# A three-mixer decoder trunk: the attention's mask moved from TensorE to VectorE, the opening's norm in other tiles, HGRN2's tail in a pool at the other end of SBUF

## The chip, the core and the metric

The kernel runs on one core of a Trainium2 chip. The core has five engines, each with its own instruction queue worked in order: TensorE (PE: matrix products, with the weight loads shown apart as PEld), VectorE (DVE), ScalarE (ACT), GpSimd (POOL) and SyncE (SP), whose queue mostly issues DMA transfers. Data lie in SBUF, 128 partitions wide; matrix products land in PSUM, which has eight banks of 128 x 512 float32 here. The metric is the device time in microseconds of one execution; a version's time is the median of several runs.

## The reference

Two layers, each: half a SwiGLU feed-forward step, a mixing step with three parallel mixers, half a second SwiGLU step. Model width 1024, sequence 512, hidden width 2816, all float32.

```python
def rms_norm(x, gain):
    inv = lax.rsqrt(jnp.mean(xf * xf, axis=-1, keepdims=True) + EPS)
    return (xf * inv) * gain

def swiglu(h, w_in, w_out):
    gate, up = jnp.split(h @ w_in, 2, axis=-1)
    return (jax.nn.silu(gate) * up) @ w_out

def fox_mixer(q, k, v, f_logit, f_bias, q_gain, k_gain):    # 8 heads of 64
    qh = rms_norm(heads(q), q_gain) * (HEAD_DIM ** -0.5)
    kh = rms_norm(heads(k), k_gain)
    cum = jnp.cumsum(jax.nn.log_sigmoid(f_logit + f_bias), axis=1)
    # block i of 128 queries:
    s = qh_i @ kh.T + (cum_i[:, None] - cum[None, :])
    s = jnp.where(qpos >= kpos, s, -1e30)
    o_i = softmax(s) @ vh

for l in range(DEPTH):
    x = x + 0.5 * swiglu(rms_norm(x, ffn1_norm[l]), ffn1_w_in[l], ffn1_w_out[l])
    h = rms_norm(x, mix_norm[l]) @ w_mix_in[l]              # 3336 columns, split over the mixers
    y = concat[short_conv(...), hgrn2(...), fox_mixer(...)] # widths 256, 256, 512
    x = x + y @ w_mix_out[l]
    x = x + 0.5 * swiglu(rms_norm(x, ffn2_norm[l]), ffn2_w_in[l], ffn2_w_out[l])
```

The short convolution is causal with three taps and two gates. HGRN2 is a gated linear recurrence with four heads, worked in chunks of 64 steps, whose output is normed per head (a mean of squares), scaled by a gain and gated by a SiLU.

## The kernel before, in words

Activations lie transposed in SBUF: features on partitions, the 512 tokens along the free dimension. A float32 product is made of three products of parts in a TensorE format: a value is split into a high part (a cast on ScalarE) and a low part (a subtraction on VectorE), and high x high, high x low and low x high are added in one PSUM bank (`mm3`, lines 318, 324, 325). Weights of the dense products come by SP into a staging tile `st` (two buffers), are split into a tile `hl` (three buffers; lines 307 and 308), and TensorE works through a stream of such pieces.

*Opening.* The first feed-forward step reads x as it arrives. `open_stream` (lines 1710 and around) turns x and works the first product while x and its weights land; the sum of squares `sqa` runs along on VectorE. Behind it the norm is made in `end_norm`: the sum is split in two tiles `sh` (`parted_norm`, line 421), summed over partitions by a product with a matrix of ones (line 430) into a bank, and ScalarE and VectorE make the reciprocal root from it (tiles `nr` and `nt`, then `inv`). Dense products use x without the norm and are multiplied by `inv` when their bank is cleared, so the second product needs no `inv`. Behind the norm `lower_bounds` loads the logits of HGRN2's lower bound by SP (line 956) into a tile `lb`. The tiles `sh` and `lb` share the tag `g1`, with two buffers. SP's loads around here stand in a written-out order, the logits' load in front of the second product's weights.

*Mixing step.* Its projections come first; those of HGRN2 lie in a pool `hg` with its working tiles, and HGRN2 runs as a generator beside the projections of the attention (`fox_qkv`): after each part of HGRN2, some pieces of dense work are recorded. Its end is the mean of squares of its output (line 1402, banks `pt`), two multiplications per half (line 1409), then five operations of VectorE over 1024 columns (lines 1412 to 1421). `fox_decay` makes the cumulated log gates with eight products (line 1440) into a `pt` bank. Then the pool closes and a pool `at` for the attention opens in its place.

The attention (`fox_attend`) runs twice, over four heads each, beside dense work: the convolution's projections and gates with the first four heads, six eighths of the output product with the last four. A head is prepared by `fox_prep` (line 1495 transposes, 1498 to 1506 splits, plus three small DMA transfers on SP and a POOL memset at 1492), then has four items, one per block of 128 queries, with 128 to 512 keys each. An item is: two products of scores into an `sc` bank (lines 1521, 1522), one that adds the mask (line 1523: an identity times a 128 x 128 matrix with -1e30 above the diagonal), the negated row maximum by VectorE (1526), Exp by ScalarE with that maximum as bias and the row sum beside it, reciprocal and scaling, transposes of the weights into a `pt` bank (1584), a split of them (1586, 1587) and products with V (1543). Scores are recorded three items ahead (`LOOK`); the tile `P`, which holds an item's Exp, has three buffers.

What sets the order: program text is recorded, and a scheduler orders each engine's instructions by the order of recording, the dependencies and its own estimates, except where the code fixes a chain with `follow`. Pools hand their space to the next pool when they close.

Of the kernel before, what the change touches and what calls it, by code (L numbers as in the profile page):

```python
# [8 lines left out]
F32 = mybir.dt.float32  # L9
# [14 lines left out]
P = 128  # L24
# [132 lines left out]
class Trunk:  # L157
# [32 lines left out]
    def build_consts(self, scratch):  # L190
# [19 lines left out]
        self.identb = c.tile([P, P], BF16, tag="identb", name="identb")  # L210
        nc.vector.tensor_copy(self.identb, self.ident)
# [206 lines left out]
    def parted_norm(self, pool, tag, bufs, keep=False):  # L418
        nc = self.nc
        hi, lo = (pool.tile([P, T], F32R, tag=tag, name=self.n("sh"), bufs=bufs) for _ in range(2))  # L420
        a, b = nc.scalar.copy(hi, self.sqacc), nc.vector.tensor_sub(lo, self.sqacc, hi)
        if keep:
            self.follow("a", a)
            self.follow("v", b)
        return hi, lo
# [133 lines left out]
    def enter(self, fp, w_in, then):  # L559
# [18 lines left out]
        parts = self.parted_norm(fp, "g1", 2, True)  # L578
# [420 lines left out]
    def mix(self, l, w, w_out, conv_w, out_gain, q_gain, k_gain, f_bias, next_gain):  # L999
# [3 lines left out]
        with tc.tile_pool(name=self.n("mix"), bufs=1) as mp:  # L1003
# [6 lines left out]
            self.mp = mp  # L1010
            og, qkg, fb, cw = col("og", 1), col("qkg", 1), col("fb", NH), col("cw", 6)
# [39 lines left out]
            with tc.tile_pool(name=self.n("hg"), bufs=1) as hp:  # L1051
                self.tt, self.tb = "t", 3
                norm = lambda: self.end_norm(
                    self.bank("pt"), hp, self.parted_norm(hp, self.tt, self.tb)
                )
                bz = features([(H_F, 256)], ("mm", "mm"), norm)
                bg = features([(H_G, 256)], ("mm", "po"))
                inv = self.inv
                z, q, sg = (
                    hp.tile([P, 2, T], F32, tag=t, name=self.n(t)) for t in ("z", "q", "sg")  # L1060
                )
                for i in range(2):
                    nc.vector.tensor_mul(z[:, i, :], bz[i], inv)
                for i in range(2):
                    nc.vector.tensor_mul(sg[:, i, :], bg[i], inv)
                self.table(SILU)
                self.act(sg, sg, AF.Silu)
                self.table(LNEXP)

                ib = hp.tile([P, 4, P], F32, tag="t", name=self.n("ib"), bufs=self.tb)  # L1070
                self.invc, self.inv2 = col("invc", 4), col("inv2", 4)
                nc.vector.tensor_mul(
                    ib, inv.rearrange("p (i t) -> p i t", i=4),
# [712 lines left out]
```

## Time and profile before

| | us |
|---|---|
| median of 3 runs | 1832.18 |
| lowest, highest | 1830.63, 1835.08 |
| the profiled execution | 1827.76 |
| its span (first to last instruction) | 1826.0 |
| TensorE busy | 1809.0 (99%) |
| VectorE busy | 1466.3 (80%) |
| ScalarE busy | 989.9 (54%) |
| mean granted TensorE clock | 0.998 |

The profile is of one execution. A line such as "L1526 DVE TENSOR_REDUCE nm<-sc" names the source line, the engine, the operation, the tile written and the tile read. The idle time behind a bar or in brackets is that of the engine just before the instruction, with what ended it. Records of matmuls overlap: one of 512 columns is shown 0.39 us long, and the next can start 0.23 us after it. The opening lies at 0 to 38 us, the mixing steps at about 390 to 600 us and 1290 to 1500 us.

### The profile page before, as it was taken

How to read it: one execution, taken by the hardware profiler on the slowest of the kernel's cores; microseconds unless marked ns; L12 is line 12 of the kernel's file. 1: busy time of each engine (PE TensorE's matmuls, PEld its weight loads, DVE VectorE, ACT ScalarE, POOL GpSimd, SP SyncE). 2: the span in 40 equal slices, each digit the busy share in tenths (PEclk: the TensorE clock that was granted, in tenths of full speed). 3: DMA queues.
4: the chain of work that ended last, by engine and by line, in shares of the span. 5: the costliest groups of instructions: out<-in, count | busy, mean ns of one | idle time of the engine just before them, and what ended most of it. 6: DMA issues, size and time to landing. Idle time of an engine off the chain costs nothing.

```text
span 1826.0 us, 34831 instructions
## 1 busy us (share of the span) xinstructions
PE 1809.0 (99%) x14345; PEld 1684.3 (92%) x14345; DVE 1466.3 (80%) x2017; ACT 989.9 (54%) x1402; POOL 169.5 (9%) x168
## 2 busy tenths in 40 slices
PE   8999999999999999999999999999999999999999
PEld 6899999899878899999889999998997788999997
DVE  8788888676797988879678887866858878888883
ACT  5455555454675565555445555555547665555551
POOL 0011020100000001112001111201000000020210
PEclk9999999999999999999999999999999999999999
DMA  5849684233322767868265787813333228677762
GB/s 147 233 109 199 171 174 113 70 88 83 87 71 92 216 141 163 191 168 174 81 193 137 162 191 194 165 64 82 83 82 82 76 93 231 162 152 195 153 137 92
DMA packets 243935, 250.94 MB, mean 137 GB/s; under 512 B 18457, under 2 KB 229153, under 8 KB 243777
## 3 DMA queue, kind: packets, MB, share of 16 engines
q1 hardware_dynamic: 189872, 182.38, 32.8%
q0 software_dynamic: 53600, 66.09, 22.7%
q8 instruction: 112, 1.84, 0.4%
q14 instruction: 47, 0.38, 0.1%
q10 hardware_dynamic: 304, 0.27, 0.0%
HBM read 223.98 MB, written 2.10 MB: 124 GB/s over the span
## 4 chain that ended last, share of the span: by engine, by line
PE 92%; DVE 3%; ACT 3%; DMA 1%; issue 1%; SPq 0%; ACTq 0%; DVEq 0%
PE mm L318 13%; PE mm L325 13%; PE mm L324 13%; PE sc L325 6%; PE sc L324 6%; PE sc L318 6%; PE pt L318 6%; PE pt L324 6%; PE pt L325 6%; PE po L318 3%; PE po L324 3%; PE po L325 3%; PE po L1543 1%; PE sc L1710 1%; PE pt L1710 1%
## 5 line engine op out<-in xcount | busy, mean ns | idle before, releaser
L786 ACT CAST hl<-w 128x1024 fp32r<-128x1024 f32 x322 | 337.5, 1051 | 317.9 <-PE mm L325 76.8
L788 DVE TENSOR_TENSOR hl<-w,hl 128x1024 fp32r<-128x1024 f32 x322 | 392.7, 1222 | 85.8 <-ACT hl L786 85.6
L307 ACT CAST hl<-st 128x512 fp32r<-128x512 f32 (+2 forms) x188 | 142.2, 756 | 190.3 <-PE po L325 67.8
L308 DVE TENSOR_TENSOR hl<-st,hl 128x512 fp32r<-128x512 f32 (+2 forms) x188 | 161.6, 860 | 100.3 <-ACT hl L307 98.6
L318 PE MATMUL mm<-xc,hl 128*128 128x256 f32 (+1 forms) x732 | 201.7, 276 | 0.5 <-ACT g L897 0.5
L325 PE MATMUL mm<-xc,hl 128*128 128x256 f32 x728 | 201.6, 277 | 0.0
L324 PE MATMUL mm<-xc,hl 128*128 128x256 f32 x728 | 201.5, 277 | 0.0
L325 PE MATMUL sc<-xc,hl 128*128 128x256 f32 x528 | 146.0, 277 | 0.0
L318 PE MATMUL sc<-xc,hl 128*128 128x256 f32 (+1 forms) x530 | 146.0, 276 | 0.0
L324 PE MATMUL sc<-xc,hl 128*128 128x256 f32 x528 | 145.9, 276 | 0.0
L318 PEld LDWEIGHTS mm<-xc,hl 128*128 128x128 f32 x732 | 137.3, 188 | 0.8 <-ACT g L897 0.7
L324 PEld LDWEIGHTS mm<-xc,hl 128*128 128x128 f32 x728 | 137.0, 188 | 0.0
L325 PEld LDWEIGHTS mm<-xc,hl 128*128 128x128 f32 x728 | 136.7, 188 | 0.1
L318 PE MATMUL pt<-xc,hl 128*128 128x256 f32 (+1 forms) x484 | 132.9, 276 | 0.0
L324 PE MATMUL pt<-xc,hl 128*128 128x256 f32 x480 | 132.7, 277 | 0.0
L325 PE MATMUL pt<-xc,hl 128*128 128x256 f32 x480 | 132.5, 276 | 0.0
L318 PE MATMUL mm<-x,hl 128*128 128x512 f32 x272 | 108.5, 399 | 6.0 <-ACT hl L307 5.6
L324 PE MATMUL mm<-x,hl 128*128 128x512 f32 x272 | 107.5, 395 | 0.0
L325 PE MATMUL mm<-x,hl 128*128 128x512 f32 x272 | 107.1, 394 | 0.0
L318 PEld LDWEIGHTS sc<-xc,hl 128*128 128x128 f32 x530 | 99.5, 188 | 0.2
L325 PEld LDWEIGHTS sc<-xc,hl 128*128 128x128 f32 x528 | 99.1, 188 | 0.1
L324 PEld LDWEIGHTS sc<-xc,hl 128*128 128x128 f32 x528 | 99.1, 188 | 0.0
(510 smaller groups left out, 5618.2 us busy)
## 6 DMA issues: line engine op xcount, KB each, us to landing
w<-in_ffn_w_in_dram SPq DMA_DIRECT2D x140, 512.0 KB, 5.2
w<-in_ffn_w_out_dram SPq DMA_DIRECT2D x64, 512.0 KB, 4.5
w<-in_ffn_w_out_dram POOLq DMA_DIRECT2D x56, 512.0 KB, 8.6
st<-in_w_mix_in_dram SPq DMA_DIRECT2D x88, 256.0 KB, 2.7
st<-in_ffn_w_in_dram SPq DMA_DIRECT2D x70, 256.0 KB, 3.3
w<-in_ffn_w_in_dram POOLq DMA_DIRECT2D x35, 512.0 KB, 8.5
w<-S POOLq DMA_DIRECT2D x35, 512.0 KB, 4.8
st<-in_ffn_w_out_dram SPq DMA_DIRECT2D x24, 512.0 KB, 4.6
```

Of the source, the lines that this page charges most:

```text
L307: a = nc.scalar.copy(hi, src[:, c : c + w])
L308: b = nc.vector.tensor_sub(lo, src[:, c : c + w], hi)
L318: i = nc.tensor.matmul(acc[:, c], ah, bh[:, c], start=first and c.start == 0, stop=False, skip_group_check=True,)
L324: nc.tensor.matmul(acc, ah, bl, start=False, stop=False, skip_group_check=True)
L325: i = nc.tensor.matmul(acc, al, bh, start=False, stop=last, skip_group_check=True)
L786: A(nc.scalar.copy(hi, src))
L788: return lambda: V(nc.vector.tensor_sub(lo, src, hi))
L1543: nc.tensor.matmul(self.ob[:, t0 + u * P : t0 + 2 * P], V[:, j, h % 4].rearrange("p a d -> p (a d)"), part[:, j, u:, :].rearrange("p i t - ...
L1710: E(nc.tensor.matmul(acc, wh[j][l][:, cols], (self.xh, self.xl)[r][k + j], start=k + j == 0 and which == 0, stop=k + j == KD - 1 and which ...
```

## The change

Four things change.

1. The opening's norm takes its two tiles `sh` from the tags `r0` and `r1` (one buffer each) and no longer from `g1`; `lb` stays in `g1`.
2. The mask's product and its identity go. A tile `zmask`, zeros and then the mask's 128 columns, is made once per layer by POOL, and VectorE's `tensor_tensor_reduce` adds the end of it to the scores, writes the negated sum into `P` and keeps the running minimum, which is the negated maximum. ScalarE's Exp reads `P` with scale -1 and no longer the bank. The operation is built as two instructions, the second of which writes the minimum.
3. HGRN2's last tiles (its four temporaries `T` and the gate `sg`) lie in a pool `hb` at SBUF's other end, its mean uses `sc` banks, and it stops once more, right after the two multiplications of line 1409. There the pool `hg` closes and the attention's pool opens in its place; its tiles wait for the tiles that they overlap and not for a whole pool. HGRN2's five last operations are recorded when the attention's fourth item is reached, and the tiles of the attention's results come in a pool `fy` in `hb`'s place after that.
4. `fox_decay` is recorded at HGRN2's first stop, and the first two heads are prepared before the last projections.

```diff
-    def parted_norm(self, pool, tag, bufs, keep=False):
+    def parted_norm(self, pool, tags, bufs, keep=False):
...
-        hi, lo = (pool.tile([P, T], F32R, tag=tag, name=self.n("sh"), bufs=bufs) for _ in range(2))
+        hi, lo = (pool.tile([P, T], F32R, tag=tag, name=self.n("sh"), bufs=bufs) for tag in tags)
...
-                    self.parted_norm(fp, "g1", 2),
+                    self.parted_norm(fp, ("r0", "r1"), 1),
...
+            self.zmask = mp.tile([P, T], BF16, tag="zm", name=self.n("zm"))
+            nc.gpsimd.memset(self.zmask[:, : T - P], 0.0)
+            nc.gpsimd.tensor_copy(self.zmask[:, T - P :], self.maskb)
...
+            left, right = ExitStack(), ExitStack()
+            hp = left.enter_context(tc.tile_pool(name=self.n("hg"), bufs=1))
+            hb = right.enter_context(tc.tile_pool(name=self.n("hb"), bufs=1, side="right"))
...
+            hgrn = self.hgrn(l, hp, hb, z, q, v, sg, og)
+            for part, n in enumerate(hgrn):
+                if n is None:
+                    break
+                if part == 0:
+                    self.fox_decay(mp, zf)
+                for _ in range(n):
+                    next(dense, None)
+            left.close()
+            ap1 = left.enter_context(
+                tc.tile_pool(name=self.n("at"), bufs=1, reuse_waits="tile")
+            )
+            for tag in ("PH", "PL"):
+                ap1.tile([P, 4, 2, P], F32R, tag=tag, name=self.n(tag), bufs=2)
+            ops = {h: self.fox_prep(ap1, h, half[0][0], qkg) for h in range(2)}
+            for _ in dense:
+                pass
...
+            def finish():
+                nonlocal ap2
+                for _ in hgrn:
+                    pass
+                right.close()
+                ap2 = right.enter_context(
+                    tc.tile_pool(name=self.n("fy"), bufs=1, side="right", reuse_waits="tile")
+                )
...
+            def beside(attend, dense, then=()):
+                for n, _ in enumerate(attend):
+                    if n == 3 and then:
+                        then()
+                    if n >= 2:
                         next(dense, None)
                 for _ in dense:
                     pass
...
+            beside(self.fox_attend(ap1, 0, half[0], qkg, ops), conv(), finish)
+            beside(self.fox_attend(ap1, 1, half[1], qkg, {}), most())
...
-        tmp = lambda: hp.tile([P, W], F32, tag="T", name=self.n("T"), bufs=4)
+        tmp = lambda: hb.tile([P, W], F32, tag="T", name=self.n("T"), bufs=4)
...
-        mb = [self.bank("pt") for _ in range(2)]
+        mb = [self.bank("sc") for _ in range(2)]
...
+        yield None
         nc.vector.tensor_scalar(t, t, scalar1=-0.5, scalar2=1.5, op0=ALU.mult, op1=ALU.add)
...
-            nc.tensor.matmul(sb[:, :n], QB[:, c], KB[:, :n], start=False, stop=False)
-            nc.tensor.matmul(sb[:, c], self.identb, self.maskb, start=False, stop=True)
+            nc.tensor.matmul(sb[:, :n], QB[:, c], KB[:, :n], start=False, stop=True)
...
-            nc.vector.tensor_reduce(nm, sb[:, :n], axis=AX.X, op=ALU.max, negate=True)
             pb = tl("P", 3)
-            self.act(pb[:, :n], sb[:, :n], AF.Exp, bias=nm, accum_out=rs)
+            nc.vector.tensor_tensor_reduce(
+                pb[:, :n], sb[:, :n], self.zmask[:, T - n :], -1.0, 3e38, ALU.add, ALU.min, nm
+            )
+            self.act(pb[:, :n], pb[:, :n], AF.Exp, bias=nm, scale=-1.0, accum_out=rs)
```

How this moves instructions is seen on three engines' queues. SP at the end of the opening, with the semaphores that each row waits for (a name such as DVE_49 is the counter of that engine, DMAHW a transfer's): before, the logits' load (`lb`), then the second product's weights (`st_504`):

```order
L1657 DMA st_296<-in_ffn_w_in_dram 128x2x256 [waits DMAHW3_49]
L956 DMA lb_457<-in_hgrn_lb_logits_dram 128x4x1 [waits DMAHW4_49,DVE_49,PE_49]
L290 DMA st_504<-in_ffn_w_in_dram 128x2x256 [waits DMAHW7_49,DMAHW6_49,DMAHW5_49]
L290 DMA st_504<-in_ffn_w_in_dram 128x2x256
L290 DMA st_534<-in_ffn_w_in_dram 128x2x256 [waits DMAHW3_49,DMAHW2_49]
```

After the change, at the same place of SP's queue:

```order
L1687 DMA st_296<-in_ffn_w_in_dram 128x2x256 [waits DMAHW3_49]
L954 DMA lb_455<-in_hgrn_lb_logits_dram 128x4x1 [waits DMAHW4_49]
L288 DMA st_502<-in_ffn_w_in_dram 128x2x256 [waits DMAHW6_49,DMAHW7_49,DMAHW5_49,DVE_49]
L288 DMA st_502<-in_ffn_w_in_dram 128x2x256
L288 DMA st_532<-in_ffn_w_in_dram 128x2x256 [waits DMAHW6_49,DMAHW5_49,DVE_49]
```

The logits' load waits for no engine any more; the weights behind it wait for VectorE's last reading of their buffer.

TensorE there: before, the opening's last products (`pt_83`), the norm's two (`po_410`), then the second product (`mm_500`):

```order
L1710 MATMUL pt_83<-x_47_300,hl_299 128x512 x3
L1710 MATMUL pt_83<-x_48_305,hl_299 128x512 x3
L430 MATMUL po_410<-sh_411,ones_mean 128x512
L430 MATMUL po_410<-sh_412,ones_mean 128x512
L318 MATMUL mm_500<-x_18_120,hl_507 128x512
```

After, from the opening's last four blocks on:

```order
L1740 MATMUL sc_80<-x_48_305,hl_299 128x512
L316 MATMUL mm_498<-x_18_120,hl_505 128x512
L322 MATMUL mm_498<-x_18_120,hl_505 128x512
L323 MATMUL mm_498<-x_18_120,hl_505 128x512
L316 MATMUL mm_499<-x_18_120,hl_505 128x512
...
L1740 MATMUL pt_83<-x_47_300,hl_299 128x512 x3
L1740 MATMUL pt_83<-x_48_305,hl_299 128x512 x3
L428 MATMUL po_408<-sh_409,ones_mean 128x512
L316 MATMUL mm_500<-x_18_120,hl_505 128x512
L428 MATMUL po_408<-sh_410,ones_mean 128x512
```

Products of the second step stand among those of the opening, and one between the norm's two.

VectorE at the attention's first items, before (`nm` the maximum, `PL` a low part, `hl` a weight's):

```order
L1529 RECIPROCAL rs_5468<-rs_5468 128x1
L1587 TENSOR_TENSOR PL_5503<-pt_5504,PH_5502 128x128
L1533 TENSOR_SCALAR P_5470<-P_5470,rs_5468 128x384
L1529 RECIPROCAL rs_5496<-rs_5496 128x1
L1526 TENSOR_REDUCE nm_5512<-sc_5508 128x1
L1587 TENSOR_TENSOR PL_5503<-pt_5519,PH_5502 128x2x128
```

After, at the same items:

```order
L1617 TENSOR_TENSOR PL_5488<-pt_5489,PH_5487 128x128
L1554 ISA P_5498,nm_5496<-sc_5493,zm_3718 128x128
L1554 ISA nm_5496 128x1
L1617 TENSOR_TENSOR PL_5488<-pt_5503,PH_5487 128x2x128
L1558 RECIPROCAL rs_5481<-rs_5481 128x1
L1441 TENSOR_TENSOR T_5240<-T_5240,T_5241 128x1024
L306 TENSOR_TENSOR hl_5757<-st_5754,hl_5757 128x512
```

The maximum has become two instructions, and HGRN2's last operations (`T`, line 1441 of the changed file) stand between the items.

TensorE at the decay, before: after the last projection's piece (`po_5242`) and the first of the convolution (`mm_5525`) come the eight products into `pt_5388`, then the first head's transposes:

```order
L325 MATMUL po_5242<-hl_5351,x_404_3711 128x256
L325 MATMUL mm_5525<-x_379_3569,hl_5529 128x512
L1440 MATMUL pt_5388<-utri,flh_5384 8x512
L1440 MATMUL pt_5388<-utri,fll_5385 8x512
...
L1440 MATMUL pt_5388<-utri,fll_5385 8x128
```

After, they stand some 900 rows earlier, in front of HGRN2's first transposes (`pt_4201`), among the attention's first projection (`mm_4167`):

```order
L322 MATMUL mm_4167<-hl_4170,x_381_3573 128x256
L1468 MATMUL pt_4153<-utri,flh_4149 8x512
L1468 MATMUL pt_4153<-utri,fll_4150 8x512
...
L1468 MATMUL pt_4153<-utri,fll_4150 8x128
L323 MATMUL mm_4167<-hl_4170,x_381_3573 128x256
L1280 MATMUL pt_4201<-ident,T_4197 128x128 x4
```

The two heads' transposes now follow HGRN2's mean directly.

More of the change, by code (lines that the diff above doesn't have):

```diff
@@ new lines, in mix @@
+            inv = self.inv
+            z, q = (hp.tile([P, 2, T], F32, tag=t, name=self.n(t)) for t in ("z", "q"))
+            sg = hb.tile([P, 2, T], F32, tag="sg", name=self.n("sg"))
+            for i in range(2):
+                nc.vector.tensor_mul(z[:, i, :], bz[i], inv)
+            for i in range(2):
+                nc.vector.tensor_mul(sg[:, i, :], bg[i], inv)
+            self.table(SILU)
+            self.act(sg, sg, AF.Silu)
+            self.table(LNEXP)
+            ib = hp.tile([P, 4, P], F32, tag="t", name=self.n("ib"), bufs=self.tb)
@@ new lines, in mix, with projections @@
+            half = [{}, {}]
+            def projections():
+                for hf in range(2):
+                    yield from self.fox_qkv(mp, hf, tokens, half)
+            dense = projections()
+            hgrn = self.hgrn(l, hp, hb, z, q, v, sg, og)
[6 more added lines that the diff above has]
+                    next(dense, None)
```

195 lines of the change are left out of this document (84 added, 111 removed).

## The prediction

> **What bounds the kernel now.** I read the profile's page first, then what TensorE waited for, then a table by stage, then the timeline at the places the change touches.
>
> ```profile
> span 1826.0 us, 34831 instructions
> ...
> PE 1809.0 (99%) x14345; PEld 1684.3 (92%) x14345; DVE 1466.3 (80%) x2017; ACT 989.9 (54%) x1402; POOL 169.5 (9%) x168
> ...
> PE 92%; DVE 3%; ACT 3%; DMA 1%; issue 1%; SPq 0%; ACTq 0%; DVEq 0%
> ...
> PE mm L318 <- ACT hl L307: 5.6, 1, 5.6
> PE pt L1440 <- DVE T L1409: 1.6, 2, 0.8
> PE mm L318 <- ACT cy L1181: 0.5, 2, 0.2
> ```
>
> TensorE carries the time: busy 99%, 92% of the chain that ended last. A change can win in two ways only, by fewer matmuls or by waits of TensorE. The largest wait is one of 5.6 us, in front of a dense product. The table by stage (PE, PEld, DVE, ACT and POOL busy, then the granted clock, DMA share and GB/s) shows where it lies, and how full VectorE is around the attention of layer 0 (layer 1 reads alike):
>
> ```profile
> 33.00:38.00 5.00, 0.00 (x0) 0.00 (x0) 3.21 (x10) 2.56 (x5) 0.00 (x0) 0.65 0.74 209
> 38.00:42.00 4.00, 3.92 (x10) 2.97 (x11) 3.82 (x6) 2.21 (x4) 0.00 (x0) 0.58 0.39 115
> 42.00:61.00 19.00, 19.00 (x85) 15.73 (x84) 17.16 (x33) 7.17 (x7) 1.44 (x1) 1.00 0.94 254
> ...
> 460.00:487.00 27.00, 26.22 (x167) 22.61 (x166) 19.48 (x33) 16.98 (x28) 0.99 (x2) 1.00 0.31 77
> 487.00:547.00 60.00, 58.77 (x340) 45.73 (x339) 55.94 (x131) 44.89 (x108) 3.24 (x6) 1.00 0.30 79
> 547.00:590.00 43.00, 42.57 (x227) 34.22 (x226) 30.40 (x62) 23.26 (x49) 0.00 (x0) 1.00 0.32 101
> ```
>
> From 33 to 38 us TensorE does nothing, and until 42 its clock is 0.58. In the attention's first 60 us VectorE is busy 93% and TensorE idles 1.23 us; ahead of it VectorE has 7.52 us free, behind it 12.6.
>
> **The opening.** The engines' timeline, SP's queue first:
>
> ```profile
> 14.96 0.88 SPq L1657 DMA_DIRECT2D st<-in_ffn_w_in_dram  x2
> 32.30 0.37 SPq L956 DMA_DIRECT2D lb<-in_hgrn_lb_logits_dram  x1
> 32.78 9.16 SPq L290 DMA_DIRECT2D st<-in_ffn_w_in_dram  x8
> ...
> SPq L956 <- DVE sh L421: 15.7, 1, 15.7
> ...
> DMA to landing us min/median/max: 2.9/3.4/7.6
> ...
> 19.99 0.67 DVE L1667 TENSOR_TENSOR hl<-st,hl 128x512 fp32r<-128x512 f32 x1
> 26.68 0.68 DVE L1667 TENSOR_TENSOR hl<-st,hl 128x512 fp32r<-128x512 f32 x1
> 30.87 0.69 DVE L421 TENSOR_TENSOR sh<-sqa,sh 128x512 fp32r<-128x512 f32 x1 [0.32 <-ACT sh L421]
> 34.64 0.69 DVE L414 SCALAR_TENSOR_TENSOR nt<-po,nt 128x512 f32<-128x512 f32 x1 [3.08 <-ACT nt L270]
> 36.98 1.05 ACT L307 CAST hl<-st 128x1024 fp32r<-128x1024 f32 x1 [2.38 <-DMA st<-in_ffn_w_in_dram]
> 38.06 1.23 DVE L308 TENSOR_TENSOR hl<-st,hl 128x1024 fp32r<-128x1024 f32 x1 [0.21 <-ACT hl L307]
> ...
> 31.87 0.63 PE L430 MATMUL po<-sh,ones_mean 128*128 128x512 f32 x2
> 38.08 0.80 PE L318 MATMUL mm<-x,hl 128*128 128x512 f32 x1 [5.58 <-ACT hl L307]
> 38.68 0.63 PE L324 MATMUL mm<-x,hl 128*128 128x512 f32 x1
> 39.10 0.63 PE L318 MATMUL mm<-x,hl 128*128 128x512 f32 x1
> 41.54 0.40 PE L325 MATMUL mm<-x,hl 128*128 128x512 f32 x1
> 41.77 0.40 PE L318 MATMUL po<-x,hl 128*128 128x512 f32 x1
> ...
> 84.57 1.23 DVE L788 TENSOR_TENSOR hl<-S,hl 128x1024 fp32r<-128x1024 f32 x1 [4.21 <-ACT hl L786]
> ```
>
> SP's queue stands from 15.9 to 32.3 on the logits' load, whose tile has the norm's buffer (tag g1), and the next weights stand behind it. They land at about 36, and TensorE idles 5.58 us. Then the clock is low: eight matmuls start from 38.08 to 41.54, in 3.46 us, where steps of 0.23 (41.54 to 41.77) would take 1.84. That is 1.6 us more, 7.2 together.
>
> With the norm in r0 and r1 the logits wait for no norm. The weights' buffer is free at 20.66 (19.99 + 0.67); 3.4 later they have landed, at 24.1, and cast (1.05) and low part (1.23) are done by about 27, while TensorE is at the opening's product until 31.87. So the whole 5.58 goes, and seven matmuls of the second product even stand ahead of the norm's second. What is late next is the norm. On VectorE its low part now stands behind that of the following weights, whose buffer comes free with the opening's last low part (27.36, and 1.23 later for the one put in front: 28.6). They land at 32.0, are cast at 33.0, lowered at 34.3, and the norm's low part ends near 35.0. TensorE arrives at 31.87 plus seven steps, 33.5. So 1.5 us of waiting come back; the rows show a low clock behind 5.58 us of idling alone, so I count it as gone. Opening: 7.2 - 1.5 = 5.7 us less. Ends: 7.2 where nothing waits; 3 where the reciprocal norm, some 3.5 us later than now, holds the banks of the third product too. I take 5.7, since VectorE's own idle of 3.08 and 4.21 us in these rows lets it come that much earlier.
>
> [...]
>
> **The mask.** 64 matmuls go, and the maximum becomes an addition with a running minimum, with a second instruction that reads it out.
>
> ```profile
> 489.06 0.23 PE L1523 MATMUL sc<-maskb,identb 128*128 128x128 bf16 x1
> 489.10 0.36 PE L1521 MATMUL sc<-KA,QA 128*128 128x256 f32 x1
> 490.62 0.23 PE L1523 MATMUL sc<-maskb,identb 128*128 128x128 bf16 x1
> 490.78 0.30 PE L1584 MATMUL pt<-ident,P 128*128 128x128 f32 x1
> 474.53 0.66 PE L1495 MATMUL pt<-ident,qk 128*128 128x128 f32 x4
> ...
> L1526 DVE TENSOR_REDUCE nm<-sc 128x1 f32<-128x512 f32 x8 | 5.5, 684 | 0.9 <-PE sc L1523 0.9
> L1182 DVE TENSOR_TENSOR cu<-mm,iv 128x512 f32<-128x512 f32 x2 | 1.4, 677 | 0.0
> L1529 DVE RECIPROCAL rs<-rs 128x1 f32<-128x1 f32 x23 | 3.6, 159 | 0.9 <-ACT P L270 0.4
> L1413 DVE TENSOR_TENSOR T<-T,T 128x1024 f32<-128x1024 f32 x1 | 1.2, 1215 | 0.0
> ```
>
> Its record is 0.23 long, but the next matmul starts 0.04 to 0.16 behind it. 64 x 0.04 = 2.6 us; the other end, 10.2, holds a load of the next weights that stays, so I take 2.6. On VectorE a product of a PSUM bank with a tile costs what the maximum costs (677 against 684 ns), so the main instruction is free; the read-out is the nearest to RECIPROCAL, one element a lane: 64 x 0.159 = 10.2 us of VectorE. Zero is its other end. (That row is of the 60 us: 23 items lie in them.) The Exp now reads SBUF and the sc bank is released one engine sooner; I cost both at nothing, beside TensorE's work.
>
> **Decay, tail and first items.** The eight decay matmuls leave their place behind HGRN2's mean, where TensorE waited 0.8 us a layer (T L1409), for HGRN2's beginning, where the same bank tag is free: 1.6 us less, or nothing if the decay's own short chain is late there. Two heads are prepared ahead, DMAs and all: on SP two negc loads and four copies stand ahead of weights that came first before, and their casts on ScalarE lie where it is busy 16.98 of 27 us; weights in two buffers and the projections' matmuls hide them. HGRN2's last five operations of VectorE, four of 1.2 us and one of 0.7, some 5.6, move from the stretch with 7.52 us free into the attention. Read-outs there: 23 x 0.159 = 3.7. VectorE's sum over both stretches is 75.4 + 3.7 = 79.1 of 87 us, so it fits if the items really begin earlier, and I take nothing for it. POOL's two instructions for the zero mask stand ahead of small loads in a queue that is 91% idle. Ends of this part, both layers: 3.3 less (the 2.44 us a layer that TensorE idles in the three rows, without the decay's) and 10.2 more (each read-out on the path).
>
> Sum: 5.7 + 2.6 + 1.6 = 9.9 us. The profiled execution took 1827.76 (span 1826.0), 4.4 under the median of 1832.18 (1830.63 to 1835.08); it would become 1817.9, the median 1822.
>
> **Rivals.**
> - *VectorE spoils the first attention half.* If the tail's 5.6 and the 3.7 of read-outs fall whole into the 60 us with 4.06 free, 5.2 a layer are over, 10.4 together, and eat the 9.9: 1833, no change; at half of it 1827. For it: 93% busy. Against it: the 7.52 us ahead. A norm that holds the third product would end near 1825 to 1828.
> - *Attention eases as well.* The bank sc is free sooner and heads 0 and 1 are ready; the 3.3 us go, and waits under 0.16 that records 0.39 long with steps of 0.23 hide: 1815 or so.
> - *Slower: VectorE held by P.* The addition writes P, which has three buffers, so VectorE's queue stops at item n+3 until TensorE has turned item n; the maximum wrote no P. Low parts of weights (L308) stand behind it, and TensorE runs dry. Turning takes up to four transposes, 0.66 us as in the row of L1495 above, and the read-out 0.16: 23 items cost 18.9 against 4.06 free, 14.8 a layer and 29.6 together, which less 9.9 is 20 slower, 1852. It decides from 0.35 us of stopping per item ((9.9 + 5.5 + 8.1) / 46 is 0.51, less 0.16 for the read-out). Against it: an item comes every 60 / 23 = 2.6 us, so three items of lead are 7.8 us, and the turning is long over.
>
> [...]
>
> **How the numbers follow.** The forecast has 0.50 (own range 1817 to 1827), eased attention 0.18, VectorE spoiled or a late norm 0.19, the slower one 0.13. Under 0.3% (5.5 us) a measurement tells nothing. Faster: the first two and a little of the third, 0.72; same 0.15; slower 0.13. The range leaves out the far ends: 1812 to 1833.
>
> **What would show it.** Right: no idle of TensorE over 2 us between 31 and 42, a clock of 1.00 there, SP's L288 loads from 21 us on; no wait at the decay's matmuls; 64 read-outs of 0.07 to 0.2 us. Wrong: VectorE busy over 58 of these 60 us in the attention's first half with more TensorE idle than 1.23; read-outs or additions at twice 0.68; VectorE waiting for PE at the additions; the third product waiting for sc or pt banks near 56 us.

## The result and the profile after

The changed kernel takes 1822.78 us (median; 1818.94 to 1823.64), the kernel before 1832.15 us measured with it. The ratio is 0.9948 with a 95% interval of 0.9933 to 0.9962, so the change made the kernel faster by 9.4 us. The forecast was 1822.0 with a range of 1812 to 1833. The sum came out right, in part by luck: the term for the decay failed, the one for the mask was too small, and what was put at nothing was not nothing; these cancelled.

The page of the profile after has the same shape as before: TensorE is the bound, with 64 matmuls fewer, and VectorE has 63 instructions more.

```profile
span 1821.3 us, 34801 instructions
...
PE 1807.4 (99%) x14281; PEld 1687.4 (93%) x14281; DVE 1466.8 (81%) x2080; ACT 990.5 (54%) x1402; POOL 170.4 (9%) x172
```

The list of what TensorE waited for (total us, times, longest), which before began with 5.6 for `hl` and 1.6 for `T`:

```profile
PE sc L1549 <- DMA KA<-KA: 1.8, 2, 0.9
PE pt L1468 <- ACT flh L1463: 1.6, 2, 0.8
...
PE sc L1549 <- DVE T L1436: 1.0, 2, 0.5
...
PE po L428 <- DVE sh L419: 0.4, 1, 0.4
```

The wait for weights in the opening is gone. The decay's wait of 0.8 us a layer is still there with another releaser: `flh`, the decay's own input, in place of `T`. Waits of the attention's first scores (`KA`, `T`) are new. The decay in the timeline of layer 0:

```profile
388.46 0.22 ACT L1463 CAST flh<-fl 128x32 fp32r<-128x32 f32 x1 [0.26 <-DVE fl L1460]
...
388.73 0.40 PE L1468 MATMUL pt<-utri,flh 128*8 128x512 f32 x1 [0.85 <-ACT flh L1463]
```

The cast ends at 388.68 us, and the product starts 0.05 later.

The opening in the timeline after: SP's queue, VectorE's low parts, TensorE.

```profile
15.87 0.47 SPq L954 DMA_DIRECT2D lb<-in_hgrn_lb_logits_dram  x1
20.71 14.35 SPq L288 DMA_DIRECT2D st<-in_ffn_w_in_dram  x8
...
26.69 1.22 DVE L306 TENSOR_TENSOR hl<-st,hl 128x1024 fp32r<-128x1024 f32 x1
32.93 1.23 DVE L306 TENSOR_TENSOR hl<-st,hl 128x1024 fp32r<-128x1024 f32 x1 [0.21 <-ACT hl L305]
34.07 0.68 DVE L419 TENSOR_TENSOR sh<-sqa,sh 128x512 fp32r<-128x512 f32 x1
...
27.96 0.50 PE L323 MATMUL mm<-x,hl 128*128 128x512 f32 x1 [0.26 <-DVE hl L306]
33.78 0.40 PE L428 MATMUL po<-sh,ones_mean 128*128 128x512 f32 x1
34.01 0.40 PE L316 MATMUL mm<-x,hl 128*128 128x512 f32 x1
34.81 0.50 PE L428 MATMUL po<-sh,ones_mean 128*128 128x512 f32 x1 [0.40 <-DVE sh L419]
```

The logits' load no longer holds SP: the weights are issued from 20.71 us on and lowered by 27.9. In place of one wait of 5.58 us TensorE has two of 0.26 and 0.40.

The table by stage (PE, PEld, DVE, ACT, POOL busy, granted clock, DMA share, GB/s), for the opening and for the three stretches that answer to 460 to 547 us before:

```profile
31.00:42.00 11.00, 10.60 (x47) 8.36 (x47) 10.32 (x31) 8.27 (x12) 0.82 (x1) 1.00 0.71 221
...
454.00:471.00 17.00, 16.28 (x182) 15.24 (x182) 10.36 (x19) 11.54 (x19) 1.04 (x2) 1.00 0.37 93
471.00:481.00 10.00, 9.25 (x47) 7.52 (x47) 9.90 (x31) 6.62 (x18) 0.52 (x1) 1.00 0.44 106
481.00:541.00 60.00, 59.46 (x320) 47.48 (x319) 55.77 (x139) 44.52 (x101) 2.60 (x5) 1.00 0.28 78
```

The clock is 1.00 in these 11 us. In the attention's 60 us VectorE is as full as before (55.77 against 55.94 us) but TensorE idles 0.54 us, not 1.23. That is no gain over the whole: in all 87 us TensorE idles 2.01 us both before (0.78 and 1.23) and after (0.72, 0.75 and 0.54). VectorE is busy 76.0 us in them, where 79.1 was forecast.

The mask's instructions on VectorE by groups (busy, mean ns), then what the additions waited for:

```profile
L1554 DVE CUSTOM_DVE_ANT_0 P<-sc,zm 128x128 f32<-128x128 f32 (+1 forms) x64 | 30.5, 482 | 6.3 <-PE pt L1614 6.0
L1554 DVE DVE_READ_ACCUMULATOR2_ANT nm<- 128x1 f32 x64 | 5.3, 83 | 0.0
```

```profile
DVE P L1554 <- PE pt L1614: 6.0, 6, 1.6
```

A read-out is 83 ns, 5.3 us in all. An addition takes as long as the maximum did (median 482 ns against 478). The records of VectorE overlap (at 492.95 us a read-out of 0.08 us and the next subtraction start together), and in the two mixing steps together its busy time does not rise (400.0 us before, 399.2 after).

Small terms are read best from one landmark: the norms' two products with the matrix of ones end one stage and begin the next. The second and third norm enclose the mixing step of layer 0, the fifth and sixth that of layer 1. Before, then after:

```profile
354.21 0.62 PE L430 MATMUL pt<-sh,ones_mean 128*128 128x512 f32 x2
609.25 0.62 PE L430 MATMUL po<-sh,ones_mean 128*128 128x512 f32 x2
1253.13 0.62 PE L430 MATMUL pt<-sh,ones_mean 128*128 128x512 f32 x2
1509.05 0.62 PE L430 MATMUL po<-sh,ones_mean 128*128 128x512 f32 x2
```

```profile
348.03 0.62 PE L428 MATMUL pt<-sh,ones_mean 128*128 128x512 f32 x2
601.71 0.62 PE L428 MATMUL po<-sh,ones_mean 128*128 128x512 f32 x2
1245.72 0.62 PE L428 MATMUL pt<-sh,ones_mean 128*128 128x512 f32 x2
1499.14 0.63 PE L428 MATMUL po<-sh,ones_mean 128*128 128x512 f32 x2
```

The second norm is 6.2 us earlier: that is the opening. The mixing steps take 253.7 and 253.4 us in place of 255.0 and 255.9, together 3.9 less. 6.2 and 3.9 are 10.1. The profiled execution itself became only 4.7 us shorter (span 1826.0 to 1821.3), since 5 us came back in the last feed-forward step, which the change does not touch; the last section shows what that is.

From norm to norm by stage (the columns as above; what TensorE is not busy of the length, it idles), before and then after:

```profile
354.21:609.25 255.04, 252.61 (x2148) 218.82 (x2147) 200.00 (x382) 152.57 (x299) 6.89 (x13) 1.00 0.32 87
1253.13:1509.05 255.92, 253.03 (x2148) 218.93 (x2147) 200.04 (x382) 152.72 (x299) 6.89 (x13) 1.00 0.32 87
```

```profile
348.03:601.71 253.68, 250.10 (x2115) 218.47 (x2114) 199.61 (x414) 153.24 (x299) 6.95 (x13) 1.00 0.33 87
1245.72:1499.14 253.42, 250.12 (x2115) 218.54 (x2114) 199.62 (x414) 153.11 (x299) 6.92 (x13) 1.00 0.33 87
```

So the 3.9 us are the sum of two opposite things: TensorE is busy 5.4 us less (505.6 to 500.2), with the mask's products gone, and idles 1.6 us more (5.3 to 6.9).

All kernels by this measure, with the time as a ratio to the kernel before on the same chip:

| kernel | second norm at | mixing steps | their sum | ratio (95% interval) |
|---|---|---|---|---|
| before | 354.2 | 255.0, 255.9 | 511.0 | 1 |
| after | 348.0 | 253.7, 253.4 | 507.1 | 0.9948 (0.9933 to 0.9962) |
| after, once more | 348.7 | 253.6, 253.3 | 506.9 | 0.9932 (0.9919 to 0.9944) |
| opening alone | 348.1 | 255.1, 254.4 | 509.6 | 0.9975 (0.9962 to 0.9988) |
| all but the opening | 354.8 | 254.7, 253.2 | 507.9 | 0.9967 (0.9954 to 0.9981) |
| mask alone | 354.6 | 254.6, 253.6 | 508.1 | 0.9962 (0.9946 to 0.9979) |
| all but the mask | 348.0 | 256.4, 256.5 | 512.8 | 0.9967 (0.9952 to 0.9981) |
| tail ahead of the attention | 348.2 | 253.3, 253.4 | 506.7 | 0.9932 (0.9908 to 0.9957) |
| decay behind the mean | 349.4 | 251.9, 252.2 | 504.1 | 0.9930 (0.9912 to 0.9949) |
| the same, once more | 349.0 | 252.3, 251.9 | 504.3 | 0.9926 (0.9913 to 0.9940) |
| decay two parts later | 349.0 | 254.5, 252.8 | 507.4 | 0.9942 (0.9929 to 0.9956) |
| that and two pieces ahead | 348.4 | 254.6, 254.7 | 509.3 | 0.9940 (0.9917 to 0.9963) |
| P with two buffers | 348.1 | 256.0, 253.6 | 509.5 | 0.9927 (0.9903 to 0.9952) |
| additions twice | 348.5 | 260.5, 260.3 | 520.8 | 1.0021 (1.0004 to 1.0039) |

Where one program was profiled twice, a step agrees to 0.5 us. Opening alone has the same mixing steps as the kernel before, and shows 1.5 us less in the second: that is the scatter to reckon with, also for the other terms that are measured against before. Where the clock fell in a step (last section) some 1.6 us more are in it. A ratio's interval is some 5 us wide, so terms of 1 to 3 us are judged by the stages.

### The profile page after: what moved, and what is told of

Read it like the earlier page. It is cut to its first block, busy times and chain, and to the rows that moved or that the text cites. A ratio compares the mean times of both kernels' runs of the same rounds, so it can differ in the third digit from the quotient of the medians.

```text
span 1821.3 us, 34801 instructions
## 1 busy us (share of the span) xinstructions
PE 1807.4 (99%) x14281; PEld 1687.4 (93%) x14281; DVE 1466.8 (81%) x2080; ACT 990.5 (54%) x1402; POOL 170.4 (9%) x172
## 3 DMA queue, kind: packets, MB, share of 16 engines
q1 hardware_dynamic: 189872, 182.38, 33.5%
## 4 chain that ended last, share of the span: by engine, by line
PE 90%; DVE 5%; ACT 3%; DMA 2%; issue 1%; SPq 0%; ACTq 0%; DVEq 0%
PE mm L323 13%; PE mm L316 13%; PE mm L322 13%; PE sc L323 6%; PE sc L322 6%; PE sc L316 6%; PE pt L322 6%; PE pt L316 6%; PE pt L323 6%; PE po L316 3%; PE po L322 3%; PE po L323 3%; PE po L1572 1%; PE pt L1614 1%; DVE hl L306 1%
## 6 DMA issues: line engine op xcount, KB each, us to landing
st<-in_w_mix_in_dram SPq DMA_DIRECT2D x88, 256.0 KB
st<-in_ffn_w_in_dram SPq DMA_DIRECT2D x70, 256.0 KB
```

## The experiments

**The opening alone.** The kernel before with one edit (and `parted_norm` made to take two tags):

```diff
-                    self.parted_norm(fp, "g1", 2),
+                    self.parted_norm(fp, ("r0", "r1"), 1),
```

> The kernel before with one edit: the opening's norm takes its two tiles from r0 and r1. Theory: the whole stall of 5.58 us and the low clock behind it (1.6 us) go, and only waits of about 1 us come in their place, as in the changed kernel's trace, where the second norm's first product starts at 348.0 us instead of 354.2. So about 6.2 us less, 1826 us, the second norm at 348.0, and the stretch from there to the third norm unchanged at 255.0. Rival one, the clock stays low behind whatever wait is left: 4.1 less, 1828. Rival two, the gain is given back later in the same feed-forward step (weights that land no earlier): the second norm's start moves by under 2 us and the time stays above 1830.

Measured: ratio 0.9975, 4.6 us less, with 6.2 inside the interval (2.2 to 7.0). Its table by stage for the opening, and its second norm:

```profile
31.00:42.00 11.00, 10.97 (x48) 8.47 (x47) 10.19 (x33) 7.43 (x11) 1.13 (x1) 1.00 0.74 230
```

```profile
348.06 0.62 PE L431 MATMUL pt<-sh,ones_mean 128*128 128x512 f32 x2
```

The clock is full and the second norm is 6.15 us earlier, the same as with the whole change. Both rivals fall: no low clock, and nothing given back inside the step.

**All but the opening.** The changed kernel with that edit undone:

```diff
-                    self.parted_norm(fp, ("r0", "r1"), 1),
+                    self.parted_norm(fp, ("g1", "g1"), 2),
```

> The changed kernel with the opening's norm back in g1, so the other three parts alone. Theory: the stall of 5.58 us is back, the second norm's first product starts at 354.2 us, and only the mixing steps gain: from norm to norm 253.7 and 253.4 us as in the changed kernel (255.0 and 256.0 before), some 3.9 us together, so about 1828.3 us. Rival, the mixing steps gained nothing and their difference was chance: 255 and 256 us, and about 1832.

Measured: ratio 0.9967, 6.0 us less (3.5 to 8.4). The second norm is back at 354.8; the mixing steps take 254.7 and 253.2 us. The first of them holds 1.6 us of low clock (last section), without which it would be 253.1. The mixing steps do gain of themselves. The two halves' times (4.6 and 6.0 less) add up to 10.6, near the whole.

**The mask alone,** in the kernel before (with `zmask` made and the identity left out, as in the change):

```diff
...
-            nc.tensor.matmul(sb[:, :n], QB[:, c], KB[:, :n], start=False, stop=False)
-            nc.tensor.matmul(sb[:, c], self.identb, self.maskb, start=False, stop=True)
+            nc.tensor.matmul(sb[:, :n], QB[:, c], KB[:, :n], start=False, stop=True)
...
-            nc.vector.tensor_reduce(nm, sb[:, :n], axis=AX.X, op=ALU.max, negate=True)
             pb = tl("P", 3)
-            self.act(pb[:, :n], sb[:, :n], AF.Exp, bias=nm, accum_out=rs)
+            nc.vector.tensor_tensor_reduce(
+                pb[:, :n], sb[:, :n], self.zmask[:, T - n :], -1.0, 3e38, ALU.add, ALU.min, nm
+            )
+            self.act(pb[:, :n], pb[:, :n], AF.Exp, bias=nm, scale=-1.0, accum_out=rs)
```

> The kernel before with the mask alone moved to VectorE (no product with the identity, addition with running minimum into P, Exp reads P); the opening, HGRN2's tail, the decay and the order of the items stay. Theory: 64 products less, 2.6 us as predicted, up to 3.7 us by the time from each one's start to the next product's in the trace; about 1829 us, and 1.3 to 1.8 us less from norm to norm in each mixing step. Read-outs at 0.084 us add 23 x 0.084 = 1.9 us to a VectorE that is busy 55.9 of 60 us. Rival, VectorE is too full without the other parts or is held by P: the mixing steps don't get shorter, additions wait for TensorE by more than the 6.0 us of the changed kernel, and the time is 1832 or more.

```profile
354.59:609.14 254.55, 250.60 (x2116) 219.00 (x2114) 199.91 (x414) 153.31 (x299) 7.14 (x13) 1.00 0.32 87
1253.12:1506.68 253.56, 250.13 (x2116) 218.34 (x2114) 200.25 (x414) 153.16 (x299) 6.87 (x13) 1.00 0.32 87
```

From norm to norm it gains 0.5 and 2.4 us, 2.9 together; against the mixing steps of opening alone, 0.6 and 0.9, or 1.4. The forecast 2.6 lies between, but not for its reason: TensorE is busy 500.7 us in the two steps, 4.9 less than before and 4.0 less than in opening alone, and it idles 7.4 us in place of 5.3 and 4.8. By its time (0.9962) it gains 7.0 us (3.9 to 9.9), more than its stages show; where the rest lies was not found, and slow matmuls as in the last section may have a part in it.

**All but the mask.** The changed kernel with those lines as they were:

> The changed kernel with the mask back on TensorE (product with the identity, maximum by one instruction, Exp from the bank); the rest as changed. Theory: 64 products more, each 0.04 to 0.06 us on TensorE's path, 2.6 to 3.7 us longer than the changed kernel's 1822.8, so 1825.4 to 1826.5, with 1.3 to 1.8 us more from norm to norm in each mixing step. Rival, read-outs and P's holding of VectorE had eaten the mask's gain: no longer than the changed kernel, 1823, or shorter.

```profile
347.96:604.31 256.35, 252.44 (x2148) 219.12 (x2146) 199.87 (x382) 152.18 (x299) 6.80 (x13) 1.00 0.32 87
1247.23:1503.71 256.48, 252.59 (x2147) 219.04 (x2146) 199.92 (x382) 152.22 (x299) 6.78 (x13) 1.00 0.32 86
```

256.4 and 256.5 us: 1.9 us more than before in sum (3.3 more than opening alone), and 5.7 more than the changed kernel. So in this trace the rearrangement without the mask costs time: TensorE is as busy as before (505.0 against 505.6 us) and idles 7.8 us, not 5.3. By the stages the mask is worth 1.4 to 2.9 us in the old order and 5.7 in the new one. In both orders it takes 4.0 to 4.9 us off TensorE's busy time; in the old one TensorE then idles 2.1 to 2.6 us more, in the new one 0.9 less. The times say the reverse, 7.0 us alone and 3.5 here (the ratio is 0.9967 and the changed kernel's 0.9948, with intervals that overlap), so that the mask is worth more in the new order is not shown. The theory had the sign, and for TensorE's busy time about half to three quarters of the size.

**The tail ahead of the attention.** The changed kernel with HGRN2's five last operations recorded before the attention and not at its fourth item:

```diff
+            finish()
             self.begin_norm(next_gain)
...
-            beside(self.fox_attend(ap1, 0, half[0], qkg, ops), conv(), finish)
+            beside(self.fox_attend(ap1, 0, half[0], qkg, ops), conv())
```

> The changed kernel with HGRN2's five last operations recorded ahead of the attention, not at its fourth item (decay, first heads, pools and mask as changed). Theory: the place of the tail was worth nothing, as predicted: VectorE has the same work in the stretches around the attention's beginning; within 1.5 us a layer, 1820 to 1826. Rival one, between the items the tail's 5.6 us hold additions up, so before them is better: 1 to 3 us a layer less, 1817 to 1821. Rival two, ahead of the attention the tail holds back the first additions with VectorE busy 9.9 of 10 us there: TensorE waits for up to 5.6 us a layer, 1828 to 1834.

Measured: 253.3 and 253.4 us, ratio 0.9932. The place of the tail is worth nothing, though it does delay the items: with it in front the first turning of an item (`P`) starts at 484.66 us, in the changed kernel at 478.23. TensorE has dense work for these 6 us: its products start 0.23 us apart for most of them, and none waits.

**P with two buffers:**

```diff
-            pb = tl("P", 3)
+            pb = tl("P", 2)
```

> The changed kernel with two buffers for P in place of three. Theory: with three buffers VectorE waits for TensorE's turning of an older item only six times (6.0 us in all, 1.6 at most), off the path; with two the addition of item n+2 stands behind the turning of item n at nearly every item, VectorE's queue stops at most of the 64 with the low parts of weights behind it, and TensorE runs dry: by 0.35 to 1.0 us an item over the 46 items of the full stretches, less the 8 us that VectorE has free, 8 to 38 us slower than the changed kernel, 1831 to 1860. Rival, the lead of the scores does not matter and VectorE's stops stay hidden: within 3 us, 1820 to 1826.

What the additions waited for in this kernel:

```profile
DVE P L1554 <- PE pt L1614: 6.2, 6, 1.2
```

Six stops and 6.2 us, as with three buffers (6, and 6.0 us); the time is 0.9927 of before. The theory that the number of buffers decides falls, and with it the mechanism behind the forecast's slower case. The long first mixing step (256.0) has a clock of 0.61 from 472 to 476 us, where the changed kernel, whose first scores start at 471.21, has 1.00; the second (253.6) is as long as in the changed kernel (253.4).

**Additions twice.** The addition and its read-out are made two times in each item:

```diff
+            for _ in range(2):
                 nc.vector.tensor_tensor_reduce(
```

> The changed kernel with the addition and its read-out made twice in each item (the second time the same values): 64 x (0.482 + 0.084) = 36.2 us of VectorE more, 18.1 in each layer, of which 23 of 32 items or 13.0 us fall into the first 60 us of the attention, where VectorE is busy 55.8 in the changed kernel and so has 4.2 free. Theory, VectorE is near its limit there but TensorE waits only for what goes over it: 13.0 - 4.2 = 8.8 us, and 5.1 more against some 9 free in the rest, so about 9 us a layer, 18 together, 1841. Rival one, each item waits for its own addition whatever VectorE has free: 18 us a layer, 1859. Rival two, three items of lead hide it: under 3 us a layer, below 1829.

The table by stage of this kernel, in the attention's first 60 us and behind it:

```profile
481.00:541.00 60.00, 56.56 (x290) 44.37 (x289) 57.07 (x161) 40.17 (x90) 2.20 (x4) 0.97 0.27 71
541.00:585.00 44.00, 42.68 (x232) 34.71 (x231) 38.80 (x109) 27.84 (x62) 0.52 (x1) 1.00 0.34 103
```

The mixing steps take 260.5 and 260.3 us, 6.8 and 6.9 more than in the changed kernel; the time is 1838.17 us. VectorE's busy time rises by 24.7 us in all (1466.8 to 1491.5), 12.3 a layer and not the 18.1 of the theory, which added up the lengths of records that overlap. So a microsecond of VectorE costs 0.55 us here: the first theory, with 6.9 a layer for the 9 it gave, and neither rival. VectorE goes up only to 57.07 us in these 60, and the rest of the work moves behind them, where it was free before (38.80 us of 44, and 32.66 in the changed kernel). TensorE idles 3.44 us, and the granted clock falls to 0.97 (0.73 from 531 to 536 us).

**The decay, three times.** First two shifts together: the decay recorded two parts of HGRN2 later, and two pieces of the convolution's dense work in front of the first scores.

```diff
-                if part == 0:
+                if part == 2:
                     self.fox_decay(mp, zf)
...
-            beside(self.fox_attend(ap1, 0, half[0], qkg, ops), conv(), finish)
+            dense = conv()
+            for _ in range(2):
+                next(dense)
+            beside(self.fox_attend(ap1, 0, half[0], qkg, ops), dense, finish)
```

> The changed kernel with two shifts of the order: the decay is recorded two parts of HGRN2 later, and two pieces of the convolution's dense work are recorded ahead of the attention's first scores. Theory: what keeps the rearranged mixing step from gaining are two waits that the rearrangement itself made: the decay's products wait 0.8 us a layer for flh, the first scores 0.9 us for the transfer of KA and 0.5 us for the multiplication T. With both covered by dense work some 2.2 us a layer go: 251.5 and 251.2 us from norm to norm in the mixing steps (253.7 and 253.4 in the changed kernel), about 1818.4 us. Rival, the waits only move on (to the first items' transposes or to weights that come later): 253 us or more in each and 1822 to 1824.

What TensorE waited for most in that kernel:

```profile
PE sc L1552 <- DVE nm L1557: 3.3, 2, 1.6
PE sc L1552 <- DVE fo L1589: 2.1, 2, 1.1
```

The waits for `flh` and `KA` are gone, and later scores wait for VectorE instead, 5.4 us in all: 254.6 and 254.7 us, the rival. The clock is 0.72 from 530 to 536 us and from 1378 to 1383, which is some 1.5 us of each step; which waits stand in front of it is not shown. Then the first shift alone:

> The changed kernel with the decay recorded two parts of HGRN2 later and nothing else, so without the two leading pieces of the run before. There the wait for flh was gone and the loss came at the scores (VectorE's nm 3.3 us, fo 2.1). Theory: the decay's wait of 0.8 us a layer goes and nothing comes for it: 252.9 and 252.6 us from norm to norm in the mixing steps (253.7 and 253.4 in the changed kernel), 1821.2 us, which the time alone can hardly tell. Rival, moving the decay also moves the weights behind it, and waits of the same size come elsewhere: 253.5 or more in each.

254.5 and 252.8 us: `flh` is no longer waited for, and layer 1 gains the 0.6. In layer 0 the first scores waited 1.4 us for `KA` and the clock fell to 0.51 from 473 to 476 us, some 1.5 us of full clock and more than that gain. By its time, 0.9942, it can't be told from the changed kernel. Last, the decay behind HGRN2's mean, as in the program's text before the change, with the mean still in `sc` banks (TensorE now meets it ahead of the last projections' pieces, at 463 us in layer 0, and before the change behind them, at 473):

```diff
-                if part == 0:
-                    self.fox_decay(mp, zf)
...
+            self.fox_decay(mp, zf)
             left.close()
```

> The changed kernel with the decay recorded again where the kernel before has it, behind HGRN2's mean, the mean's banks staying sc. Theory: in the kernel before it was the pt banks of the mean that held the decay up for 0.8 us, and flh had long been made; with the mean in sc banks the products wait for nothing there, so the bank tag and not the decay's place was worth the 0.8 us: no row of the decay's products waiting for flh or T over 0.3 us, 252.9 and 252.6 us from norm to norm. But the heads' preparation needs the decay's result for KB by a transfer, which then starts some 1 us before its use: rival, the first scores wait for that transfer by 1 to 3 us a layer more, 254.5 us or more.

251.9 and 252.2 us, 3.0 less than the changed kernel in sum. The same beside the changed kernel:

> The changed kernel once more, beside the next one on the same chip. Theory and rival alike: 253.7 and 253.4 us from norm to norm in the mixing steps, 6.2 us earlier at the second norm than before, some 9.5 us less than the kernel before.

> The changed kernel with the decay behind HGRN2's mean once more, beside the changed kernel on the same chip. Theory: the decay's move to HGRN2's beginning is a loss of its own, 3 us in both layers (251.9 and 252.2 us from norm to norm against 253.7 and 253.4), so about 3 us less than the changed kernel and 12.5 less than before. Rival, the single trace was chance: 253 us or more in each mixing step, and no less than the changed kernel by its median.

The second time, its norms and its largest wait:

```profile
348.99 0.62 PE L428 MATMUL pt<-sh,ones_mean 128*128 128x512 f32 x2
601.33 0.62 PE L428 MATMUL po<-sh,ones_mean 128*128 128x512 f32 x2
1244.85 0.62 PE L428 MATMUL pt<-sh,ones_mean 128*128 128x512 f32 x2
1496.77 0.62 PE L428 MATMUL po<-sh,ones_mean 128*128 128x512 f32 x2
```

```profile
PE pt L1522 <- DVE negc L1473: 2.4, 2, 1.2
```

252.3 and 251.9 us against 253.6 and 253.3: 2.6 us less, in all four steps the same sign. No row has the decay's products waiting, but the second head's transposes behind them wait 1.2 us, by the releaser (`negc`) for the bank that the decay holds. The waits for `KA` and `T` are no longer among the large ones. In the two layers 4.4 us of waits are gone (1.6 for `flh`, 2.8 for `KA` and `T`) and 2.4 have come. The medians are 1817.42 us (1816.75 to 1820.38) and 1818.99 us (1816.99 to 1821.69), ratios to before 0.9926 and 0.9932: the same sign, but their ranges overlap, so the time alone does not settle it. It is the lowest median of all these kernels, 14.7 us under the kernel before on its chip.

## Why the prediction was right or wrong

- *The opening, 5.7 us less: right, 6.2.* "the whole 5.58 goes", and the low clock with it. The 1.5 us that "come back" were 0.26 and 0.40. The norm's low part ended at 34.75 us, where 35.0 was forecast; TensorE arrived later than the forecast's 33.5, since the opening's own products ended only at 33.8 with seven products of the next step in between (34.01 and a step of 0.23 is 34.24). No bank of the third product was waited for. The clock stayed at 1.00 behind these two waits; that it is low behind the 5.58 us alone, as the forecast read from its rows, does not hold in the runs of the last section, where it fell once behind 1.07 and 0.37 us.
- *The mask, 2.6 us less: the right way, but too small for TensorE's busy time (4.0 to 4.9).* The forecast took the low end of its rows, 0.04 us a product; the 64 steps from start to start add up to 3.7 us in the trace before, 0.06 each, and the busy time fell by 0.06 to 0.08 each. That alone the step gained only 1.4 to 2.9 is owed to more idling there, whose cause is not shown. The main instruction is as long as the maximum, as forecast. "the read-out is the nearest to RECIPROCAL" was wrong by a factor of two, 83 ns and not 159, and VectorE's busy time did not rise by it.
- *The decay, "1.6 us less, or nothing if the decay's own short chain is late there": the step that failed.* That chain is late: the products wait 0.85 us for `flh`. So the wait moved, and 1.6 us were not gained. More than that, the move costs 2.6 to 3.0 us against the old place with the mean in `sc` banks. The forecast argued from the bank ("the same bank tag is free"); it named the late chain as an end but worked out no time for it. Nor did the mean's other banks make the old place free of waiting: 1.2 us a layer stand behind the decay there, at the second head's transposes. The old place wins because the waits for `flh`, `KA` and `T` are absent; why `KA` and `T` come in time there is not shown, and the bank tag was not tried by itself.
- *Tail and first items, nothing taken: right for the tail, wrong for the rest.* The tail's place is worth nothing, as shown by recording it in front. "weights in two buffers and the projections' matmuls hide them" was wrong: behind the heads prepared ahead the first scores wait 1.8 us for `KA`'s transfer and 1.0 for `T`, both layers together. With the decay behind the mean the rest is a gain: 504.2 us against 508.1 for the mask alone, 3.9 less, for the heads prepared ahead, the pools and the mean's banks together. They were not tried apart. That is near the end of 3.3 less that the forecast had set.
- *The sum.* Forecast: 5.7 + 2.6 + 1.6 = 9.9 less. By the stages: 6.2 for the opening, 1.4 to 2.9 for the mask, 3.9 for first items, pools and banks, less 2.8 for the decay's move: 8.7 to 10.2, against 10.1 between the two traces' stages and 9.4 (13.1 beside its second measurement) between the medians. This sum is no test of its terms, since the last two are differences of the same traces and must add up. What tests the forecast is TensorE itself: for the mixing steps it had 2.6 less work and 1.6 less waiting, 4.2 in all; they show 5.4 less busy and 1.6 more idle, 3.9 less. That 3.9 is so near 4.2 is luck.
- *The rivals.* VectorE does not spoil the attention: as full as before, with TensorE idle 0.54 us in place of 1.23. The doubled additions show that it could, at 0.55 us for each microsecond. The attention eases in these 60 us alone; what TensorE idles less there it idles more ahead of them. VectorE held by P falls: the holding is real (six times, 6.0 us) but rare, and one buffer less changes it by 0.2 us. Each addition is two instructions, 64 rows of each, but the rival's 1833 does not come true: the read-outs did not lengthen VectorE's busy time (400.0 us in the two mixing steps before, 399.2 after).

## What to carry to other kernels

When work is moved to where its output bank is free, ask for each of its operands when it is ready there: a wait that is removed at one semaphore can stand at the next one, as it did here (0.8 us a layer for `T` before, 0.8 for `flh` after). Try the parts of such a change one by one, since here the old place, with the other parts kept, was better than the move. And split a gain into less work and less waiting: here the work fell by more than the time. Where an effect is smaller than the scatter between executions, compare the distance between two landmarks of the program around the edit, not the whole span.

## What the runs showed of the hardware

A matmul stream ran 4% slower in one execution than in two others, at a recorded clock of 1.00. Ninety microseconds of the last feed-forward step, before, after, and after once more:

```profile
1600.00:1690.00 90.00, 90.00 (x796) 90.00 (x796) 76.61 (x79) 47.60 (x54) 14.35 (x12) 1.00 0.78 176
```

```profile
1590.00:1680.00 90.00, 90.00 (x766) 90.00 (x765) 73.38 (x76) 46.28 (x52) 14.34 (x12) 1.00 0.77 172
```

```profile
1590.00:1680.00 90.00, 90.00 (x796) 90.00 (x796) 76.58 (x80) 47.39 (x53) 14.34 (x12) 1.00 0.79 176
```

TensorE is busy without a gap each time, with 796 matmuls or 766: a step of 0.113 or of 0.1175 us. Missing records are not the reason: from the last norm shown to the end both traces have 2504 matmuls, in 313.0 us of busy time before and 318.2 after. It comes in stretches of 20 to 120 us: where most windows of ten microseconds hold 90 or 91 of these matmuls, there are 87 or 88 in each from 980 to 1000 and from 1180 to 1210 us before, and from 650 to 670 and from 1560 to 1680 us in the first profile of the changed kernel, which lost 3.4 us over the ninety microseconds above. Its cause is not shown. Between the two profiles of the changed kernel it lies where the spans differ: 1821.3 and 1816.6 us, of which this last stretch takes 322.2 and 317.5.

And the clock fell behind short waits. The attention's first scores in the kernel with all but the opening, by stage and in the timeline:

```profile
476.00:480.00 4.00, 2.56 (x11) 1.84 (x10) 3.85 (x7) 3.10 (x6) 0.00 (x0) 0.91 0.52 131
480.00:483.00 3.00, 3.00 (x9) 2.29 (x9) 2.92 (x9) 1.07 (x3) 0.00 (x0) 0.55 0.50 128
```

```profile
477.65 0.30 PE L1549 MATMUL sc<-KA,QA 128*128 128x128 f32 x1 [1.07 <-DMA KA<-KA]
478.46 0.38 PE L1549 MATMUL sc<-KA,QA 128*128 128x256 f32 x1 [0.37 <-DVE T L1436]
```

TensorE idled 1.44 of 4 us, and then the clock stood at 0.55 for 3 us, some 1.6 us lost (eight steps of 0.43 in place of 0.23). The same place in the changed kernel kept a clock of 1.00 with waits of 0.93 and 0.54 us, and with 1.05 and 0.54 in its second profile. With the decay two parts later, waits of 1.35 and 0.43 us stood in front of the clock of 0.51. So short waits close together went ahead of a low clock in two of these four executions, the longest of them 1.07 and 1.35 us, and what decides is not shown.
